# Both MLP products as seven half-size products instead of eight, with the activations kept in DRAM

## The chip, the cores and the metric

The kernel runs on one core of a Trainium2 chip. The metric is the device time of one execution in microseconds (us). Several engines work side by side, each on its own list of instructions: TensorE (PE, matmuls; its weight loads are shown as PEld), VectorE (DVE), ScalarE (ACT), GpSimd (POOL) and SyncE (SP), which here issues the DMA transfers. They wait for each other through semaphores.

## The reference

One decoder layer on 512 tokens of width 2048, in float32: three token mixers, gates, an output projection, and then the part that the change is about. All of it ends in one norm:

```python
x = x + merged @ w_out[l]
h = rmsnorm(x, norm_mlp[l])
x = x + jnp.square(jax.nn.relu(h @ mlp_w1[l])) @ mlp_w2[l]   # 2048 -> 8192 -> 2048
return rmsnorm(x, final_norm)                                # (1, 512, 2048)
```

## The kernel before

Activations are feature-major: a tile holds 128 features on the partitions and the 512 tokens along the free axis, so 16 tiles make up x. A float32 product is made from three products of a reduced type (fp32r): every operand is split exactly into a high and a low half, and hi·hi, hi·lo and lo·hi are added up in PSUM. `wtiles` (L723) brings 512 KB of weights (eight 128x128 tiles) by one DMA into `raw`, ScalarE casts it to `hi` (L731) and VectorE subtracts to get `lo` (L732); each of the three buffers has 3 copies. `gemm` (L735) runs the three matmuls of each weight tile (L748 to L750): the weight tile is stationary, 512 tokens move through.

The stages that matter are the last ones (L1118 to L1210). The output projection makes 16 tiles `wo0` to `wo15`; each is added to x on VectorE, scaled and split into `hh` (high, ScalarE) and `ho` (low, VectorE), and squared for the norm, whose factor R is multiplied in after the first MLP product. The MLP runs in 8 pieces c of 1024 hidden features: 8 tiles of the first product (each 16 weight tiles), ReLU (ScalarE), two multiplications and a split (`ah`, `al`), and then 16 tiles of the second product (each 8 weight tiles), each added to x. The last half piece is run in two halves of the tokens (256 columns), so that the final norm of the first half lies beside the matmuls of the second.

The order of TensorE's instructions is the order of the code (`manual_schedule`). The other engines' lists are ordered by the framework's scheduler from dependences and priorities; weight preparation has a high priority (`wprio`), and buffer counts set how far it runs ahead.

## Time and profile before

| what | us |
|---|---|
| runs: median (lowest to highest), 3 runs | 3062.14 (3059.55 to 3068.38) |
| profiled execution: span | 3059.8 |
| of it: everything up to the last product of w_out | 1646 |
| the MLP's matmuls | 1397 |
| from the last matmul of the MLP on | 17 |

The profile gives the span of one execution, and no time of its own for what lies around it. Its span is 2.3 us below the median of the runs and within their spread. Times in the trace count from the span's start. A row of the timeline is: start, length, engine, line, operation, output<-inputs, count, and in brackets how long the engine was idle before it and what released it. A group's row gives the count, the busy time, the mean length of one in ns and the idle time before them. A matmul's length contains its way through the array; the next one starts earlier, so rates are read from starts.

### The profile page before, as it was taken

What the parts mean: (1) busy time and instruction counts of PE and PEld (TensorE: products, weight loads), DVE (VectorE), ACT (ScalarE), POOL (GpSimd) and SP (SyncE); (2) the same over time, 40 slices, a digit from 0 to 9 for tenths busy, and PEclk for the clock granted to TensorE, in tenths of its full rate; (3) what the DMA queues carried; (4) which work ended last, traced back from release to release, by engine and by line L of the source; (5) the groups of instructions that cost most, each with busy time, mean ns of one, the idle gap of its engine ahead of it and who ended that gap; (6) DMA issues with size and microseconds to landing.
All of it is one profiled execution on the core that took longest, in us unless ns stands there. A gap on an engine that the chain in (4) does not pass through costs nothing.

```text
span 3059.8 us, 36455 instructions
## 1 busy us (share of the span) xinstructions
PE 3001.3 (98%) x14143; PEld 2468.2 (81%) x14143; DVE 1557.3 (51%) x2350; ACT 989.0 (32%) x1224; POOL 336.8 (11%) x572
## 2 busy tenths in 40 slices
PE   8999988999999999999999999999999999999997
PEld 7888776788877777888888888888888888888887
DVE  7766888855664555555334334333333434333335
ACT  6554121234662233422223222122222212222235
POOL 1001766530000000011110000000000000000003
PEclk9999988999999999999999999999999999999999
DMA  5345333445337163655432333333233323323334
GB/s 181 124 162 185 114 103 98 136 131 166 102 103 190 55 186 97 229 165 170 157 98 94 97 99 96 99 98 97 97 97 97 97 96 97 97 96 97 97 97 151
DMA packets 172638, 370.72 MB, mean 121 GB/s; under 512 B 63377, under 2 KB 74385, under 8 KB 171665
## 3 DMA queue, kind: packets, MB, share of 16 engines
q1 hardware_dynamic: 172464, 368.38, 38.2%
q8 instruction: 112, 1.84, 0.3%
q14 instruction: 62, 0.50, 0.1%
HBM read 318.81 MB, written 44.58 MB: 119 GB/s over the span
## 4 chain that ended last, share of the span: by engine, by line
PE 85%; DVE 6%; POOL 3%; DMA 3%; SPq 1%; issue 1%; ACT 0%; DVEq 0%; ACTq 0%; POOLq 0%
PE w L748 15%; PE w L749 15%; PE w L750 15%; PE gt L748 5%; PE gt L750 5%; PE gt L749 5%; PE z L748 2%; PE z L750 2%; PE z L749 2%; PE wo L750 2%; PE up L748 2%; PE wo L748 2%; PE up L750 2%; PE up L749 2%; PE wo L749 2%
## 5 line engine op out<-in xcount | busy, mean ns | idle before, releaser
L731 ACT CAST whw<-wrw 128x1024 fp32r<-128x1024 f32 x264 | 278.0, 1053 | 885.8 <-PE w L749 872.4
L32 DVE TENSOR_TENSOR wlw<-wrw,whw 128x1024 fp32r<-128x1024 f32 x264 | 324.1, 1227 | 405.2 <-ACT whw L731 405.2
L748 PE MATMUL w<-ah,whw 128*128 128x512 f32 (+1 forms) x1088 | 409.9, 377 | 0.1
L750 PE MATMUL w<-ah,wlw 128*128 128x512 f32 (+1 forms) x1088 | 409.7, 377 | 0.0
L749 PE MATMUL w<-al,whw 128*128 128x512 f32 (+1 forms) x1088 | 409.7, 377 | 0.0
L748 PE MATMUL w<-hh,whw 128*128 128x512 f32 x1024 | 398.7, 389 | 0.0
L750 PE MATMUL w<-hh,wlw 128*128 128x512 f32 x1024 | 398.4, 389 | 0.0
L749 PE MATMUL w<-ho,whw 128*128 128x512 f32 x1024 | 398.4, 389 | 0.0
L748 PE MATMUL gt<-uh,whgt 128*128 128x512 f32 x768 | 310.6, 404 | 2.8 <-DVE gz L26 2.8
L750 PE MATMUL gt<-uh,wlgt 128*128 128x512 f32 x768 | 300.6, 391 | 2.0 <-DVE wlgt L32 2.0
L749 PE MATMUL gt<-ul,whgt 128*128 128x512 f32 x768 | 300.2, 391 | 0.0
L29 DVE TENSOR_TENSOR x<-x,w 128x512 f32<-128x512 f32 (+1 forms) x136 | 89.2, 656 | 388.0 <-PE w L750 388.0
L748 PE MATMUL z<-uh,whin 128*128 128x512 f32 x608 | 243.7, 401 | 11.8 <-DVE zs L26 11.8
L750 PE MATMUL z<-uh,wlin 128*128 128x512 f32 x608 | 241.0, 396 | 8.1 <-DVE wlin L32 8.1
L749 PE MATMUL z<-ul,whin 128*128 128x512 f32 x608 | 240.0, 395 | 0.0
L748 PEld LDWEIGHTS w<-ah,whw 128*128 128x128 f32 x1088 | 204.7, 188 | 37.7 <-issue 0.2
L749 PEld LDWEIGHTS w<-al,whw 128*128 128x128 f32 x1088 | 204.7, 188 | 37.5
L750 PEld LDWEIGHTS w<-ah,wlw 128*128 128x128 f32 x1088 | 204.7, 188 | 37.4
L748 PEld LDWEIGHTS w<-hh,whw 128*128 128x128 f32 x1024 | 192.2, 188 | 40.2 <-issue 0.2
L749 PEld LDWEIGHTS w<-ho,whw 128*128 128x128 f32 x1024 | 192.2, 188 | 40.1 <-issue 0.2
L750 PEld LDWEIGHTS w<-hh,wlw 128*128 128x128 f32 x1024 | 192.2, 188 | 39.9
L29 POOL TENSOR_TENSOR acc<-acc,sq 128x512 f32<-128x512 f32 x29 | 49.7, 1713 | 1521.7 <-ACT sq L830 1490.7
(442 smaller groups left out, 4577.8 us busy)
## 6 DMA issues: line engine op xcount, KB each, us to landing
wrw<-in_w SPq DMA_DIRECT2D x264, 512.0 KB, 3.6
wrgt<-in_w_in SPq DMA_DIRECT2D x96, 512.0 KB, 4.0
wrin<-in_w_in SPq DMA_DIRECT2D x76, 512.0 KB, 3.6
wrup<-in_w_up SPq DMA_DIRECT2D x32, 512.0 KB, 4.0
wrwo<-in_w_out SPq DMA_DIRECT2D x32, 512.0 KB, 3.6
gd<-gz SPq DMA_DIRECT2D x48, 256.0 KB, 2.2
gl<-gd SPq DMA_DIRECT2D x48, 256.0 KB, 3.1
zd<-zs SPq DMA_DIRECT2D x21, 256.0 KB, 2.0
```

What stands on the lines that cost most here:

```text
L29: (eng or self.nc.vector).tensor_tensor(out, a, b, ALU.add)
L32: (eng or self.nc.vector).tensor_tensor(out, a, b, ALU.subtract)
L731: nc.scalar.copy(hi, raw)
L748: nc.tensor.matmul(ps, hi[:, ws], xh, start=first, stop=False)
L749: nc.tensor.matmul(ps, hi[:, ws], xl, start=False, stop=False)
L750: nc.tensor.matmul(ps, lo[:, ws], xh, start=False, stop=last)
```

## The change

Both MLP products are cut in 2x2 blocks and formed by the Strassen–Winograd scheme: seven block products in place of eight, from sums of blocks. For a product A·B with blocks A11, A12, A21, A22 of the weights, the sums of weights are built up in one buffer (A11, +A12, +A22, +A21) and a second (B: A22, +A12), each 128x1024 sum being split into high and low as a weight was before (`wsums`).

- The projection `wo` runs in the order 0, 8, 1, 9, ...; `hsums(k)` forms four blocks and four differences or sums of h (128x256 each) in the buffer `hG` and splits seven of them into `hch`, `hcl` (128x1792). This happens for k = 0 to 2 inside the projection, and for k = 3 to 7 behind it, in memory that the projection's operands leave.
- x goes token-major: 64 transposes on TensorE, copies on ScalarE, and 16 DMAs to DRAM (`x1d`); they come back for the second product as `xT0` to `xT3`. The norm's factor is one number per token, R2.
- First product: 32 units u, each with 7 products x 8 weight tiles x 3 matmuls of 256 columns. `w1_out` combines the products, squares the ReLU and stores 512 KB of hidden activations to DRAM (`hid`).
- Second product: token-major. Activations are stationary (128 tokens), weights move (512 columns). For each of 8 pieces c and 2 halves n of the output: 7 products x 2 token tiles x 24 matmuls. `hidden(u)` brings one stored tile back (`aG`, 2 buffers), GpSimd forms the four sums, ScalarE and VectorE split 128x1792 (`ah`, `al`, 6 buffers each). `out2` adds each product from PSUM into xT on VectorE, scaled by R2.
- The final norm is one factor per token; w2 is laid out anew on the host.

Comments and docstrings are dropped as well. The diff, cut to its core:

```diff
+    ORDER = (1, 5, 6, 3, 7, 2, 4)
+    def sums(self, G, hi, lo, eng=None):
+        a21, a11, a22, a12, s1, s2, s3, s4 = (G[:, q] for q in range(8))
+        self.sub(s1, a21, a22, eng)
+        self.sub(s2, s1, a11, eng)
+        self.sub(s3, a11, a21, eng)
+        self.add(s4, s2, a12, eng)
+        self.hl(G[:, 1:].rearrange("p q t -> p (q t)"), hi, lo)
+    def wsums(self, name, B, pool, order=None):
...
+        def acc(c, q):
+            t = self.wp.tile([P, 1024], F32, name=f"w{c}{q}{name}", tag="wraw", bufs=self.wraw)
+            nc.sync.dma_start(t, B[q])
+            self.add(at[c], at[c], t)
+            return at[c]
+        how = {1: lambda: load("A", "11"), 5: lambda: acc("A", "12"), 6: lambda: acc("A", "22"),
+               4: lambda: acc("A", "21"), 3: lambda: load("B", "22"), 7: lambda: acc("B", "12"),
+               2: lambda: load("C", "21")}
+        for i in order or self.ORDER:
+            with self.tc.high_priority(self.wprio):
+                x = how[i]()
...
+                nc.scalar.copy(hi, x)
+                self.sub(lo, x, hi)
+            yield i, hi, lo
+    def w1_out(self, u, i, bank, keep, pool, hid):
+        with self.tc.high_priority(2 * self.wprio):
+            if i in (1, 5, 6):
+                keep[i] = pool.tile([P, 256], F32, name=f"pk{i}_{u}", tag=f"pk{i}", bufs=2)
+                nc.scalar.copy(keep[i], bank[self.BANK[i]])
...
+            if i == 7:
+                self.sub(y[:, 2], keep[5], bank["a"])
...
+            elif i == 4:
+                nc.scalar.copy(y[:, 0], bank["a"])
+                f = y.rearrange("p q t -> p (q t)")
+                self.stt(f, f, 0.0, f, ALU.max, ALU.mult)
+                nc.sync.dma_start(hid, f)
-                    for j in range(NT):
-                        pt = self.gps(f"wo{j}")
-                        self.run(self.gemm(f"wo{j}", d["w_out"][j], [(pt, NT)], m))
-                        self.add(x1[j], x1[j], pt)
...
-                        nc.scalar.activation(hi, x1[j], AF.Copy, scale=col("norm_mlp", j))
-                        self.stt(lo, x1[j], col("norm_mlp", j), hi, ALU.mult, ALU.subtract)
...
+                def hsums(k):
+                    G = fp.tile([P, 8, 256], F32, name=f"hG{k}", tag="hG")
+                    for q in range(2):
+                        nc.scalar.activation(G[:, 2 * q:2 * q + 2].rearrange("p q t -> p (q t)"), x1[k + 8 * q], AF.Copy,
+                                             scale=col("norm_mlp", k + 8 * q))
+                    self.sums(G, *hc[k])
+                for n, j in enumerate(q for k in range(8) for q in (k, k + 8)):
...
+                    if j in (8, 9, 10):
+                        hsums(j - 8)
+                trunk.close()
...
+                for k in range(3, 8):
+                    hsums(k)
...
+                gen = self.wsums("u0", w1_quadrants(0), None, (1, 5, 2, 6, 3, 7, 4))
+                bank, keep = banks(0), {}
+                three = [next(gen) for _ in range(3)]
+                for i, *w in three:
+                    self.w1_mm(bank[self.BANK[i]], i, w, hc, range(3))
...
+                    for i, *w in three:
+                        self.w1_mm(bank[self.BANK[i]], i, w, hc, range(3, 8))
+                        self.w1_out(0, i, bank, keep, mp, hid[0])
...
+                    def hidden(u):
+                        with tc.high_priority(2 * self.wprio):
+                            G = mp.tile([P, 8, 256], F32, name=f"aG{u}", tag="aG", bufs=2)
+                            nc.sync.dma_start(G[:, 0:4].rearrange("p q t -> p (q t)"), hid[u])
+                            r = [mp.tile([P, 1792], F32R, name=f"a{q}{u}", tag=f"a{q}", bufs=6) for q in "hl"]
+                            self.sums(G, *r, nc.gpsimd)
+                        return r
...
+                            if n == 0:
+                                for ph in range(2):
+                                    for _ in range(2):
+                                        i, *w = next(gens[ph])
+                                        for t in range(2):
+                                            mm2(bank[self.BANK[i]][t], i, w, aa, ph, t)
+                                            if ph:
+                                                out2(i, n, bank[self.BANK[i]][t], t)
+                            elif c < 7:
+                                nxt = [hidden(4 * c + 4 + u) for u in range(4)]
+                            for (i, *w), (_, *w1) in zip(*gens):
+                                for t in range(2):
+                                    ps = bank[self.BANK[i]][t]
+                                    mm2(ps, i, w, aa, 0, t)
+                                    mm2(ps, i, w1, aa, 1, t)
+                                    out2(i, n, ps, t)
```

Three places in the engines' lists are spoken of below. The first is VectorE's list at the turn from the output projection to the first MLP product. Before, the last split (`ho15`) and the preparation of weights (`wl...`):

```order
L32 TENSOR_TENSOR wlw1_0_0_13456<-wrw1_0_0_13453,whw1_0_0_13455 128x1024
L42 SCALAR_TENSOR_TENSOR ho11_13170<-x1_2_12342,pcol_75,hh11_13169 128x512
L42 SCALAR_TENSOR_TENSOR ho12_13239<-x1_3_12343,pcol_75,hh12_13238 128x512
L42 SCALAR_TENSOR_TENSOR ho13_13308<-x1_3_12343,pcol_75,hh13_13307 128x512
L42 SCALAR_TENSOR_TENSOR ho14_13377<-x1_3_12343,pcol_75,hh14_13376 128x512
L32 TENSOR_TENSOR wlw1_0_8_13494<-wrw1_0_8_13491,whw1_0_8_13493 128x1024
L29 TENSOR_TENSOR x1_3_12343<-x1_3_12343,wo15_13383 128x512
L32 TENSOR_TENSOR wlw1_1_0_13534<-wrw1_1_0_13531,whw1_1_0_13533 128x1024
L42 SCALAR_TENSOR_TENSOR ho15_13446<-x1_3_12343,pcol_75,hh15_13445 128x512
```

And now, the sums and splits of k = 3 to 7 in `hG` behind the last addition to x (the pieces for k = 5, 6 and 7 follow in the same way):

```order
L30 TENSOR_TENSOR x1_3_12355<-x1_3_12355,wo15_13360 128x512
L33 TENSOR_TENSOR wlu0_2_13541<-wCu0_13538,whu0_2_13540 128x1024
L33 TENSOR_TENSOR hcl3_13431<-hG3_13440,hch3_13430 128x1792
L33 TENSOR_TENSOR hG4_13449<-hG4_13449 128x256 x3
L30 TENSOR_TENSOR hG4_13449<-hG4_13449 128x256
L33 TENSOR_TENSOR hcl4_13433<-hG4_13449,hch4_13432 128x1792
L33 TENSOR_TENSOR hG5_13458<-hG5_13458 128x256 x3
L30 TENSOR_TENSOR hG5_13458<-hG5_13458 128x256
L33 TENSOR_TENSOR hcl5_13435<-hG5_13458,hch5_13434 128x1792
```

One split of 128x512 after `wo15` has become five splits of 128x1792 with the sums of four of them.

The second place is SP's list at the turn from the first to the second product. Before, loads of weights alone:

```order
L728 DMA wrw1_7_0_13945<-in_w1 128x1024
L728 DMA wrw1_7_8_13975<-in_w1 128x1024
L728 DMA wrw2_0_0_0_14015<-in_w2 128x1024
L728 DMA wrw2_0_1_0_14039<-in_w2 128x1024
L728 DMA wrw2_0_2_0_14078<-in_w2 128x1024
```

And now, behind the store of the last hidden tile (`hid31`) and the load of `aG0`, the hidden tile `aG1`, weights, and x and the final norm's factors (1 MB each), and `aG2` (`aG3` follows it):

```order
L1288 DMA aG1_21050<-hid1_13486 128x1024
L791 DMA wAv000_21086<-in_w2 128x1024
L791 DMA wAv001_21123<-in_w2 128x1024
L791 DMA wAv010_21406<-in_w2 128x1024
L791 DMA wAv011_21412<-in_w2 128x1024
L1279 DMA xT0_21028<-x1d0_13517 128x2048
L1279 DMA xT1_21029<-x1d1_13518 128x2048
L1279 DMA xT2_21030<-x1d2_13519 128x2048
L1279 DMA xT3_21031<-x1d3_13520 128x2048
L1281 DMA gfin_21036<-in_final_row 128x2048
L796 DMA wA22v001_21171<-in_w2 128x1024
L1288 DMA aG2_21060<-hid2_13487 128x1024
```

The hidden tiles 2 and 3, needed by the first piece, stand behind ten transfers, five of them of 1 MB, which were not there before.

The third is VectorE's list around the start of piece c = 2 of the second product. Before, at the start of a piece:

```order
L26 TENSOR_TENSOR a31_17197<-a31_17197,R_81 128x512
L26 TENSOR_TENSOR a31_17197<-a31_17197 128x512
L32 TENSOR_TENSOR al31_17202<-a31_17197,ah31_17201 128x512
L29 TENSOR_TENSOR x1_0_12340<-x1_0_12340,w2_3_0_17205 128x512
L32 TENSOR_TENSOR wlw2_3_3_0_17305<-wrw2_3_3_0_17302,whw2_3_3_0_17304 128x1024
L29 TENSOR_TENSOR x1_0_12340<-x1_0_12340,w2_3_1_17206 128x512
```

And now (`wl...` split of a weight sum, `wA...` a sum of weights, `al...` split of hidden tiles, `xT...` a product added to x):

```order
L43 SCALAR_TENSOR_TENSOR xT0_21028<-oa110_21960,R2_13521,xT0_21028 128x512
L30 TENSOR_TENSOR wAv200_22286<-wAv200_22286,wA12v200_22304 128x1024
L33 TENSOR_TENSOR al10_21989<-aG10_21986,ah10_21988 128x1792
L43 SCALAR_TENSOR_TENSOR xT1_21029<-oa111_21961,R2_13521,xT1_21029 128x512
L33 TENSOR_TENSOR al11_21999<-aG11_21996,ah11_21998 128x1792
L33 TENSOR_TENSOR wlv200_5_22308<-wAv200_22286,whv200_5_22307 128x1024
L33 TENSOR_TENSOR wlv201_1_22326<-wAv201_22323,whv201_1_22325 128x1024
L30 TENSOR_TENSOR wAv200_22286<-wAv200_22286,wA22v200_22364 128x1024
L30 TENSOR_TENSOR wAv201_22323<-wAv201_22323,wA12v201_22343 128x1024
L33 TENSOR_TENSOR al12_22569<-aG12_22566,ah12_22568 128x1792
L43 SCALAR_TENSOR_TENSOR xT2_21030<-oa200_22280,R2_13521,xT2_21030 128x512
L33 TENSOR_TENSOR wlv201_5_22347<-wAv201_22323,whv201_5_22346 128x1024
```

After these the list goes on with `xT3`, `wlv200_6`, `al13`, `wAv201` (+A22), `xT0`, `xT1` and `wlv201_6`. Two per-tile steps between matmuls (an addition and a split) have become a mix of sums, splits of weights, splits of hidden tiles and additions to x, in one list.

## Rows read from the trace of the kernel before

**Rows 1.** the page's head.

```profile
span 3059.8 us, 36455 instructions
```

**Rows 2.** windows by stage: us, busy PE PEld DVE ACT POOL, PEclk, DMA, GB/s.

```profile
0.00:1646.00 1646.00, 1603.10 (x7799) 1303.58 (x7800) 1000.36 (x1721) 606.59 (x772) 304.00 (x544) 0.99 0.45 140
1646.00:3043.00 1397.00, 1396.93 (x6342) 1164.16 (x6341) 548.61 (x613) 379.41 (x448) 27.28 (x22) 1.00 0.31 99
3043.00:3060.00 17.00, 1.30 (x6) 0.49 (x4) 8.34 (x17) 3.04 (x5) 5.49 (x7) 0.67 0.49 168
```

**Rows 3.** groups by form of the MLP stage: busy us, mean ns, idle before.

```profile
L748 PE MATMUL w<-hh,whw 128*128 128x512 f32 x1024 | 398.7, 389 | 0.0
L748 PE MATMUL w<-ah,whw 128*128 128x512 f32 x960 | 373.4, 389 | 0.0
L748 PE MATMUL w<-ah,whw 128*128 128x256 f32 x128 | 36.5, 285 | 0.1
L32 DVE TENSOR_TENSOR wlw<-wrw,whw 128x1024 fp32r<-128x1024 f32 x262 | 321.6, 1227 | 404.4 <-ACT whw L731 404.4
L29 DVE TENSOR_TENSOR x<-x,w 128x512 f32<-128x512 f32 x120 | 82.5, 688 | 382.7 <-PE w L750 382.7
L731 ACT CAST whw<-wrw 128x1024 fp32r<-128x1024 f32 x262 | 275.9, 1053 | 880.0 <-PE w L749 872.4 <-PE wo L749 4.4 <-issue 3.2
L810 ACT CAST ah<-a 128x512 fp32r<-128x512 f32 x64 | 39.7, 621 | 136.1 <-DVE a L26 136.1
```

**Rows 4.** timeline of PE, first and 57th of 57 starts with 512 columns.

```profile
2959.73 0.39 PE L748 MATMUL w<-ah,whw 128*128 128x512 f32 x1
...
2972.43 0.39 PE L750 MATMUL w<-ah,wlw 128*128 128x512 f32 x1
```

**Rows 5.** timeline of PE, first and 53rd of 53 starts with 256 columns.

```profile
2999.72 0.28 PE L748 MATMUL w<-ah,whw 128*128 128x256 f32 x1
...
3005.97 0.28 PE L749 MATMUL w<-al,whw 128*128 128x256 f32 x1
```

**Rows 6.** timeline of DVE (start, us) around the start of GpSimd's multiplies.

```profile
3027.63 0.42 DVE L26 TENSOR_TENSOR acc<-acc,acc 128x256 f32<-128x256 f32 x1
3027.97 0.41 DVE L29 TENSOR_TENSOR x<-x,w 128x256 f32<-128x256 f32 x1
3028.64 1.22 DVE L32 TENSOR_TENSOR wlw<-wrw,whw 128x1024 fp32r<-128x1024 f32 x1
3029.77 0.97 DVE L29 TENSOR_TENSOR acc<-acc,sq 128x256 f32<-128x256 f32 x1
3030.99 1.43 DVE L32 TENSOR_TENSOR wlw<-wrw,whw 128x1024 fp32r<-128x1024 f32 x1
```

**Rows 7.** timeline of POOL: the final multiplies of 128x256.

```profile
3028.85 16.08 POOL L26 TENSOR_TENSOR x<-x,rt 128x256 f32<-128x256 f32 x16 [29.64 <-DVE rt L42]
3048.92 3.55 POOL L26 TENSOR_TENSOR x<-x,rt 128x256 f32<-128x256 f32 x4 [3.98 <-DVE rt L42]
```

**Rows 8.** DMA issues of the whole span: KB each, us to landing.

```profile
wrw<-in_w SPq DMA_DIRECT2D x264, 512.0 KB, 3.6
x<-in_xT SPq DMA_DIRECT2D x4, 1024.0 KB, 9.9
```

**Rows 9.** timeline of ACT at the turn from w_out to w1.

```profile
1646.72 0.72 ACT L1137 ACTIVATE hh<-x,pcol 128x512 fp32r<-128x512 f32 x1
1647.35 0.62 ACT L830 ACTIVATE sq<-x 128x512 f32<-128x512 f32 x1
```

**Rows 10.** windows in the mixers' stage, columns as in rows 2.

```profile
435.00:440.00 5.00, 2.91 (x16) 2.75 (x16) 5.00 (x10) 0.66 (x2) 4.84 (x6) 0.74 0.45 153
440.00:445.00 5.00, 4.91 (x19) 4.55 (x20) 2.18 (x2) 0.66 (x2) 4.65 (x16) 0.50 0.39 124
```

**Rows 11.** timeline of the tail.

```profile
3047.49 0.42 DVE L42 SCALAR_TENSOR_TENSOR acc<-rt 128x256 f32<-128x256 f32 x1 [2.21 <-ACT rt L371]
3047.95 0.42 DVE L26 TENSOR_TENSOR acc<-acc,acc 128x256 f32<-128x256 f32 x1
```

More of the change, by code (lines that the diff above doesn't have):

```diff
@@ L1 @@
+import contextlib
 import math
@@ new lines, in main @@
+                x1 = [xq[j // 4][:, j % 4] for j in range(NT)]
+                for q in (0, 2, 1, 3):
+                    nc.sync.dma_start(xq[q], d["xT"][4 * q:4 * q + 4].rearrange("j p t -> p j t"))
+                acc = R
+                def hsums(k):
[4 more added lines that the diff above has]
+                    self.sums(G, *hc[k])
@@ new lines, in main @@
+                pm = self.gps("pms")
+                for t in range(4):
+                    nc.tensor.matmul(pm[:, 2 * t:2 * t + 2], acc[:, t * P:t * P + P], self.onesD[:, 0:2], start=True, stop=True)
+                self.ts(R2, pm[:, 0:8:2], 1e-6, ALU.add)
+                nc.vector.reciprocal(R2, R2)
+                front.close()
+                with mixpool("w1", "right") as mp:
+                    for i, *w in three:
+                        self.w1_mm(bank[self.BANK[i]], i, w, hc, range(3, 8))
+                        self.w1_out(0, i, bank, keep, mp, hid[0])
+                    for i, *w in gen:
+                        self.w1_mm(bank[self.BANK[i]], i, w, hc, range(8))
+                        self.w1_out(0, i, bank, keep, mp, hid[0])
+                    for u in range(1, 32):
+                        bank, keep = banks(u), {}
+                        for i, *w in self.wsums(f"u{u}", w1_quadrants(u), mp):
+                            self.w1_mm(bank[self.BANK[i]], i, w, hc, range(8))
+                            self.w1_out(u, i, bank, keep, mp, hid[u])
```

220 lines of the change are left out of this document (130 added, 90 removed).

## The prediction

> **What bounds the kernel now.** I read the stages first. Up to 1646 us the lists of before and after are the same until the first product of w_out, and little of what follows in that stage moves. The MLP's 1397.00 us hold 1396.93 us of busy TensorE at a granted clock of 1.00 (2.4 GHz), while VectorE is busy for 548.61 us of them, 39%, and ScalarE for 379.41; a tail of 17 us follows [rows 2]. So a matmul taken away here is worth its rate, as long as the other engines keep up. They do now: VectorE's splits of weights are preceded by 404.4 us of idle time, ended by ScalarE's casts, which themselves wait 872.4 us for TensorE to release buffers [rows 3]. That idle VectorE time is what the change spends.
>
> **TensorE's part.** From the first to the 57th start with 512 columns, 12.70 us pass, so one takes 0.2268 us [rows 4]; with 256 columns 52 steps take 6.25 us, 0.1202 us each [rows 5]. Before: 3072 matmuls of 512 columns in the first product (696.7 us), 2880 of 512 and 384 of 256 in the second (653.2 + 46.2 = 699.4 us); counts from [rows 3], three lines alike for each. After: the first product has 32 x 7 x 8 x 3 = 5376 of 256 columns, 646.2 us, so 50.5 us less, not an eighth, since the half as wide matmul costs more than half. The second has 8 pieces x 2 halves x 7 products x 2 token tiles x 12 = 2688 of 512 columns, 609.6 us, 89.8 us less. If all else were hidden, 140 us would be gained.
>
> The Trainium skill ("TensorE: Matmul & The Clock Gate", section "Back-to-back issue gap") gives an isolated gap of N/2.4 + 2.5 ns, 109 ns for 256 columns and 216 for 512. By that the first product would save 77 us (5376 x 0.1092 against 3072 x 0.2158). The two starts measured here are 11 ns longer each, which weighs twice as often on the narrow ones, and I go by the rows.
>
> **VectorE's prices.** 128x1024 from SBUF takes 1.23 us [rows 3] and the next starts 1.13 after it; 128x256 takes 0.42, next after 0.34 [rows 6], next dependent one after 0.46 [rows 11]; 128x512 takes 0.69 [rows 3], so I count 0.60. For 128x1792, which no row has, a straight line through 0.688 and 1.227 gives 2.04, step 1.94; ScalarE's cast by 0.621 and 1.053 gives 1.70 [rows 3]. From below, a split of 1792 can't cost less than the 1.23 of 1024; from above, two of 1024, 2.46. I take the line.
>
> **First product.** Per unit VectorE does 7 splits and 4 sums of 1024, the squared ReLU of 1024 and three additions of 256: 12 x 1.14 + 3 x 0.34 = 14.7 us, beside 168 x 0.1202 = 20.2 us of TensorE. Hidden, but one chain is tight: sum 6 and its split stand in the list behind additions that wait for PSUM. I allow 5 us in all (0 to 15).
>
> **Second product, the crux.** In one half n of a piece TensorE works 168 x 0.2268 = 38.1 us. VectorE has 22 operations of 1024 (14 splits, 8 sums), 25.1 us, and 14 additions from PSUM, 8.4: 33.5 us. In each piece four splits of 1792 come on top, 7.8 us. So VectorE has 74.8 us of work in 76.2: nothing is left for waiting. And it stands badly: all four splits are in the first half. Around the start of a piece (time 0: last matmul of the piece before), the list runs from the addition xT0, which waits for TensorE until -2.72, over a weights' sum and al10 (0.60 + 1.14 + 1.94) to +0.96, then xT1, al11, al12, al13, eight operations of 1024 and four more additions: 3.0 + 5.8 + 9.1 = 17.9 us, to 18.9. TensorE needs the last of these, the low half of sum 6, after 4 x 2.72 + 1.8 = 12.7 us. So at least 6.2 us are lost per piece. On top, al12 waits for a chain that starts only when al10 frees its buffer: DMA 3.6 [rows 8], four GpSimd operations 3.6 to 4.0 (four take 3.55 [rows 7]), a cast 1.70. Against VectorE's own work up to there this leaves two waits that I put at 0.9 and 2.4 us (an estimate from these lengths and the list; nothing to 4 us together). GpSimd contention comes next: with GpSimd running from 3028.85 us, a split takes 1.43 instead of 1.22 and a 128x256 addition of two SBUF inputs 0.97 instead of 0.42 [rows 6, 7]. The operations concerned lose 0.2 each, 1.5 us per piece, together 11 us for each of pieces 1 to 7: 77 us. Lower bound 6.2 (43 us), upper bound below.
>
> A gap in TensorE's work may cost clock. In the mixers' stage, after a stretch with 2.91 us busy of 5, the granted clock was 0.50 (1.2 GHz) in the next 5 us although TensorE was busy for 4.91 [rows 10]. The waits here are of 1 to 3 us in a row of busy groups; I take 1 us per piece, 7 us; nothing to 3 us each. The second halves have 33.5 of 38.1 us, but two splits come 0.1 to 0.4 us before their need: 5 us in all (0 to 12). ScalarE's casts (14 x 1.05, two of 1.70 on the mean: 18 us per half) and GpSimd's 16 operations per piece cost nothing of their own beyond this, beside 38.1 us of matmuls.
>
> **Turn from w_out to the first product.** Here nothing stood still before. Now k = 3 to 7 share one buffer hG, so scaling (0.63 + 0.72 [rows 9]), three dependent sums (0.46 + 0.46 + 0.42, 1.4 with the wake-up), cast 1.70 and split 2.04 come one after another, 6.5 us for each of four, after 5.6 us for the first: 31.8 us. Then 30 matmuls remain (3.6 us). Of the first product's matmuls 72, those of k = 0 to 2 of three products, can run before (8.7 us), so 27 us are lost, and I take 28 for a stretch at half clock (22 to 35).
>
> What I cost at nothing there: 64 transposes, the copies and the 16 stores of x, which lie in that same wait; the sums for k = 0 to 2, about 3.4 us of VectorE each, which lie beside w_out's matmuls in place of the splits `ho`.
>
> **Turn to the second product.** aG2 and aG3 stand on SP's list behind ten transfers. Four loads of 1 MB back to back had a median landing of 9.9 us [rows 8], so some 2.2 us per MB and about 23 us for these, with the weights among them; with sums on GpSimd (8 in 7.1), cast and split, al3 is ready about 36 us after the last store, and the work TensorE can do until then is 48 matmuls, 10.9 us, behind the first hidden tiles. Loss 30 us, and 6 for the first piece's list as above: 36 (25 to 50).
>
> **Tail.** The last norm is per token, with its additions beside matmuls: 11 us for 17, and 3 us of waits in the last group: 14.
>
> **Sum.** 1646 + 28 + 646 + 5 + 610 + 36 + 77 + 7 + 5 + 14 = 3074 us of span, against 3059.8 [rows 1]. The median of the runs before is 2.3 us above its span; I predict 3076.
>
> **Rivals.**
> 1. *TensorE stays the bound* (faster). Weight splits run up to three buffers ahead and the waits in VectorE's list fall into slack that I did not see. For it speaks that VectorE's work fits into the time in every stage. With no loss per piece and both turns at their low ends: 3074 - 89 - 6 - 11 = 2968; with the 6.2 us per piece still lost, 3011. Against it: 74.8 of 76.2 us is no slack.
> 2. *VectorE and GpSimd block each other* (slower still). If each of a piece's 16 GpSimd operations holds VectorE up by 0.55 us, as the 128x256 addition was, that is 8.8 us per piece, 7.3 more than I counted, 58 us: 3134. The Trainium skill ("SBUF — State Buffer", section "SBUF: two separate sides") has it as an exclusive lock between GpSimd and a VectorE operation with two SBUF inputs, where the second waits to the end. As a mechanism of this kernel, 16 x 0.89 = 14.2 us per piece from the uncontended row [rows 7] would make it 102 us more, 3178. The rows bear the lock out in part: 1.43 for 1.22 is far less than a whole 0.89.
> 3. *The loads come late* (slower). Each half of the second product reads 14 loads of 512 KB and, on the mean, two hidden tiles, 8.4 MB in 38.1 us: 220 GB/s where the stage moved 99 [rows 2]. Three raw buffers serve 12 of these loads, so one is used anew every 9.5 us; if a landing grows from 3.6 us towards 6, the sums begin to wait for it. At 0.25 to 0.5 us for each of 224 loads that is 56 to 112 us: 3132 to 3188. Against it: the shares of the DMA engines in [rows 2] are under a half.
>
> **How the numbers follow.** Forecast 0.49 (3045 to 3105), rival 1 0.28, rival 2 0.14, rival 3 0.09. Range 3000 to 3135: below it lie rival 1's best cases, above it the full lock and the late loads. This kernel's measurement can tell 0.3%, 9 us, from no change. Faster than 3053: rival 1 and 0.05 of the forecast, 0.33. Between 3053 and 3071: 0.16. Slower: 0.51.
>
> **What would show it.** Right: w1 units of 20.2 us at clock 1.00; TensorE idle for about 28 us at the first turn, ended by VectorE's hcl; idle behind al2/al3 at the second; per piece one idle stretch of some 10 us in the first half, ended by VectorE's wl splits, and none to speak of in the second. Wrong: VectorE busy below 90% in the second product (rival 1), its 1024 operations well above 1.23 us (rival 2), or idle ended by DMA (rival 3).

## The result, and the profile after

| | median, us (lowest to highest) | ratio to before, 95% interval |
|---|---|---|
| before, 4 runs beside it | 3064.17 (3059.55 to 3068.38) | |
| after, 4 runs | 3110.16 (3105.58 to 3117.95) | 1.015 (1.0132 to 1.0168) |

The change makes the kernel 46 us slower. I had forecast slower, 3076 (3000 to 3135): the side was right, but only under a third of the loss (14 of 46 us). The profiled execution of after, and its windows by stage with the columns of [rows 2]:

```profile
span 3108.5 us, 41754 instructions
```

```profile
0.00:1647.70 1647.70, 1601.89 (x7797) 1302.02 (x7798) 1012.19 (x1726) 607.73 (x767) 303.71 (x544) 0.98 0.45 139
1647.70:1676.60 28.90, 18.23 (x101) 15.33 (x100) 16.93 (x22) 22.57 (x31) 1.72 (x1) 0.67 0.49 175
1676.60:2323.70 647.10, 644.98 (x5350) 639.96 (x5350) 483.65 (x477) 269.59 (x349) 0.00 (x0) 1.00 0.63 206
2323.70:2337.10 13.40, 0.18 (x3) 0.02 (x1) 3.58 (x4) 3.11 (x3) 5.85 (x8) 0.61 0.82 306
2337.10:3085.20 748.10, 670.52 (x2688) 520.90 (x2688) 644.07 (x610) 296.19 (x287) 153.60 (x121) 0.95 0.54 180
3085.20:3108.50 23.30, 0.16 (x1) 0.00 (x0) 12.92 (x25) 8.63 (x16) 0.00 (x0) 0.55 0.44 180
```

In [rows 2] TensorE was busy for all but 0.07 us of the MLP. Now the first product runs as before (644.98 of 647.10 us, clock 1.00), but there is a hole at each turn (rows 2 and 4 here), the second product has 77.6 us without TensorE and a granted clock of 0.95, and the tail is 23.3 us. VectorE is busy for 644.07 of 748.10 us there.

**The first turn.** TensorE's list after the projection, with the bracket naming what ended the idle time, and VectorE's splits beside it:

```profile
1655.66 1.14 PE L1251 MATMUL xt<-cst,x 128*128 128x128 f32 x8 [2.18 <-ACT xs L1253]
1674.89 1.84 PE L1257 MATMUL pms<-cst,R 128*128 128x2 f32 x8 [1.54 <-ACT xs L1253]
1676.59 0.56 PE L817 MATMUL ha<-hch,whu 128*128 128x256 f32 x1
```

```profile
1657.71 2.03 DVE L33 TENSOR_TENSOR hcl<-hG,hch 128x1792 fp32r<-128x1792 f32 x1 [1.85 <-ACT hch L888]
1664.30 2.03 DVE L33 TENSOR_TENSOR hcl<-hG,hch 128x1792 fp32r<-128x1792 f32 x1 [1.81 <-ACT hch L888]
1677.53 2.03 DVE L33 TENSOR_TENSOR hcl<-hG,hch 128x1792 fp32r<-128x1792 f32 x1 [0.39 <-ACT hch L888]
```

Two chains run side by side. The splits come every 6.6 us (1657.71 to 1664.30), as forecast. But TensorE stands in front of the transposes of x, and each group waits for ScalarE's copy of the one before; only behind the last (1674.89) does its list come back to the matmuls, at 1676.59. It reaches those that need the last split when that one ends (1677.53 + 2.03 = 1679.56), 31.8 us after the first product's first matmul.

**The second turn.** TensorE, then SP's issues:

```profile
2337.09 0.79 PE L1299 MATMUL oa<-whv,ah 128*128 128x512 f32 x1 [13.22 <-ACT ah L888]
2358.53 0.80 PE L1299 MATMUL oa<-whv,ah 128*128 128x512 f32 x1 [9.06 <-ACT ah L888]
```

```profile
2325.94 1.25 SPq L1288 DMA_DIRECT2D aG<-hid  x2
2329.73 2.91 SPq L1279 DMA_DIRECT2D xT<-x1d  x4
2338.09 0.33 SPq L796 DMA_DIRECT2D wA22v<-in_w  x1
2340.55 2.26 SPq L1288 DMA_DIRECT2D aG<-hid  x2
```

The third and fourth hidden tiles are asked for at 2340.55, although the queue took its entry before them at 2338.09. The buffers say why: `aG` has two, and the first is free only when `al0` is made, at 2340.53 (read from these times, not tried by itself). Then the load itself takes 11.84 us, where one takes 3.29 at the start of piece c = 1 below. Its place in the chain of waits, and the window in which it is under way (columns as above):

```profile
2340.55 11.84 DMA aG<-hid
```

```profile
2340.50:2352.40 11.90, 8.61 (x23) 6.03 (x23) 9.72 (x9) 3.86 (x4) 0.00 (x0) 0.73 1.01 414
```

The DMA engines have no room there (share 1.01, 414 GB/s). In front of this load stand those of x and of the final norm's factors, 1 MB each, which land one after another, 2.5 us apart, up to 2349.84; it lands at 2352.39. In accum2 (below), where x is asked for behind the third hidden tile, that tile lands in 3.3 us, and the first half of the first piece takes 54.8 us instead of 66.0, among other edits:

```profile
aG<-hid SPq DMA_DIRECT2D x1, 512.0 KB, 3.3
```

**A piece of the second product.** The chain of waits at the start of piece c = 1 (start, length, what; "issue" is time for which the profile shows no wait):

```profile
2443.26 2.04 DVE al L33
2445.30 0.02 issue
2445.32 3.29 DMA aG<-hid
...
2448.74 4.21 POOL aG L33 x3
...
2453.03 1.61 POOL aG L30
...
2454.66 1.71 ACT ah L888
...
2456.39 1.93 DVE al L33
```

From the end of the split that frees the buffer (2445.30) to the end of the next tile's own (2458.32) lie 13 us of DMA, GpSimd, ScalarE and VectorE in turn, and what TensorE waits for stands behind it on VectorE: 

```profile
2460.44 0.79 PE L1299 MATMUL oc<-wlv,ah 128*128 128x512 f32 x1 [2.35 <-DVE wlv L33]
2461.46 0.63 PE L1299 MATMUL oc<-whv,al 128*128 128x512 f32 x1
2461.89 0.63 PE L1299 MATMUL oc<-wlv,ah 128*128 128x512 f32 x1
```

After the wait of 2.35 us a matmul starts every 0.43 us, and the granted clock from 2460.4 to 2466.1 is 0.50 (1.2 GHz):

```profile
2460.40:2466.10 5.70, 5.66 (x13) 4.46 (x14) 5.70 (x5) 0.70 (x2) 3.95 (x2) 0.50 0.35 122
```

From piece 1 on, 7 to 20 matmuls of each first half run so. The rate at full clock, first and 95th of 95 starts, for [rows 4]:

```profile
2486.79 0.39 PE L1299 MATMUL ob<-whv,ah 128*128 128x512 f32 x1
...
2508.73 0.40 PE L1299 MATMUL oa<-whv,al 128*128 128x512 f32 x1
```

21.94 us over 94 steps are 0.2334 us each (0.2327 on the mean over the stage's steps without a wait), against 0.2268 before.

### The profile page after: what moved, and what is told of

It is laid out like the page before. It is cut to its first block, busy times and chain, and to the rows that moved or that the text cites. A ratio compares the mean times of both kernels' runs of the same rounds, so it can differ in the third digit from the quotient of the medians.

```text
span 3108.5 us, 41754 instructions
## 1 busy us (share of the span) xinstructions
PE 2936.0 (94%) x15933; PEld 2478.2 (80%) x15933; DVE 2173.3 (70%) x2863; ACT 1207.8 (39%) x1451; POOL 464.9 (15%) x673
## 3 DMA queue, kind: packets, MB, share of 16 engines
q1 hardware_dynamic: 208000, 507.86, 50.7%
## 4 chain that ended last, share of the span: by engine, by line
PE 70%; DVE 13%; DMA 7%; issue 3%; POOL 3%; ACT 3%; SPq 1%; DVEq 0%; ACTq 0%; POOLq 0%
PE ha L817 11%; PE oa L1299 6%; PE hc L817 5%; PE gt L749 5%; PE gt L751 5%; PE gt L750 5%; PE oc L1299 3%; PE hb L817 3%; PE z L749 3%; PE z L751 2%; PE z L750 2%; DVE wlv L33 2%; PE ob L1299 2%; DMA wA21v<-in_w 2%; PE wo L749 2%
## 5 line engine op out<-in xcount | busy, mean ns | idle before, releaser
L817 PE MATMUL ha<-hch,wlu 128*128 128x256 f32 x1024 | 292.1, 285 | 1.2 <-DVE wlu L33 1.1
L817 PE MATMUL ha<-hch,whu 128*128 128x256 f32 x1024 | 289.1, 282 | 0.9 <-DVE hy L33 0.9
L817 PE MATMUL ha<-hcl,whu 128*128 128x256 f32 x1024 | 289.0, 282 | 0.0
L1299 PE MATMUL oa<-whv,ah 128*128 128x512 f32 x512 | 206.5, 403 | 22.4 <-ACT ah L888 22.3
L1299 PE MATMUL oa<-wlv,ah 128*128 128x512 f32 x512 | 206.5, 403 | 10.2 <-DVE wlv L33 9.3
L807 ACT CAST whv<-wAv 128x1024 fp32r<-128x1024 f32 x128 | 132.9, 1049 | 198.3 <-DVE wAv L30 69.4
L1299 PE MATMUL oa<-whv,al 128*128 128x512 f32 x512 | 205.3, 401 | 4.5 <-DVE al L33 4.5
L33 DVE TENSOR_TENSOR wlu<-wAu,whu 128x1024 fp32r<-128x1024 f32 x128 | 154.0, 1222 | 78.5 <-ACT whu L807 78.5
L817 PEld LDWEIGHTS ha<-hch,wlu 128*128 128x128 f32 x1024 | 194.4, 190 | 5.8 <-DVE wlu L33 2.0
L817 PEld LDWEIGHTS ha<-hch,whu 128*128 128x128 f32 x1024 | 194.1, 190 | 1.1 <-ACT whu L807 1.1
L817 PEld LDWEIGHTS ha<-hcl,whu 128*128 128x128 f32 x1024 | 193.9, 189 | 0.2 <-DVE hcl L33 0.2
```

The lines of the kernel that those rows point to most:

```text
L33: (eng or self.nc.vector).tensor_tensor(out, a, b, ALU.subtract)
L807: nc.scalar.copy(hi, x)
L817: self.nc.tensor.matmul(ps, w[a][:, ws], hc[k][b][:, g], start=i in (1, 5, 2) and k == 0 and q == 0, stop=k == 7 and q == 2, skip_group_ch ...
L1299: nc.tensor.matmul(ps, x[a][:, g], w[b][:, ws], start=i in (1, 5, 2) and ph + p + q == 0, stop=ph + p + q == 4, skip_group_check=True)
```

## The experiments

All ratios are to the kernel before on the same chip (median 3063 to 3066). "Halves" are the times between the first matmuls of the two halves n of each piece; in after the first piece has 66.0 and 40.3, the other seven 45.3 to 53.3 and 39.5 to 40.7. Ranges below are of pieces 1 to 7, and of the second halves without the very last.

**dvesum: no GpSimd.**

```diff
-                            self.sums(G, *r, nc.gpsimd)
+                            self.sums(G, *r, nc.vector)
```

> Only edit: the four sums of each hidden tile in the second product run on VectorE instead of GpSimd. Theory 1 (GpSimd and VectorE hold each other up: VectorE's weight sums take 1.75 us instead of 1.22 beside GpSimd in the changed kernel, and GpSimd's four sums 5.9 us): VectorE gains 0.34 x 16 = 5.4 us of work per piece but loses the holding up and the chain to the third hidden tile gets some 4 us shorter; the first half of a piece falls from 52.6 to 46 to 49 us, the whole to 3065 to 3085. Rival (VectorE's list is simply too long in the first half): the first half stays at 52 to 55 us, the whole at 3105 to 3130.

Measured: 3107.01 us, 1.0141 (1.0125 to 1.0156); first halves 50.7 to 53.1 in the middle pieces. Piece 1 of after, then of dvesum:

```profile
2443.40:2495.90 52.50, 45.15 (x170) 34.14 (x169) 46.88 (x41) 20.07 (x18) 22.54 (x16) 0.90 0.54 180
```

```profile
2444.20:2495.60 51.40, 42.72 (x169) 33.14 (x168) 48.01 (x57) 19.99 (x18) 0.00 (x0) 0.93 0.56 184
```

With GpSimd at 0 instead of 22.54 us the half is 1.1 us shorter. VectorE takes over the 16 sums (0.42 us each) and is busy for only 1.1 us more, because its other operations no longer stretch: over pieces 1 to 7 of after they take 2.9 us per piece longer than here. So contention has a price, a third of the 8.8 us of rival 2, and most of what dvesum saves of it the 16 sums use up. The run excludes the size of rival 2, not contention.

**static_w2: no weight work in the second product.** After its first half, no weight is loaded, summed or split; the last ones are used again.

```diff
-                            gens = [self.wsums(f"v{c}{n}{ph}", bq(ph), mp, order) for ph in range(2)]
+                            if c == n == 0:
+                                gens = [self.wsums(f"v{c}{n}{ph}", bq(ph), mp, order) for ph in range(2)]
+                            else:
+                                gens = [iter([(i, *kept[ph]) for i in order]) for ph in range(2)]
```

> Left out: the loads, sums and splits of the second product's weights from its second half-piece on; all later products use one kept pair of weight tiles, so the result is another one. The hidden tiles' loads, sums and splits and the additions to x stay. Any theory by which VectorE's, ScalarE's or the loads' work for weights holds TensorE up expects every later half at TensorE's own rate: 168 x 0.2327 = 39.1 us, the whole near 3012. If the longer step of 0.2327 us (0.2267 in the kernel before) comes from weights being written beside the matmuls, it falls to 0.2267 and the halves to 38.1 us, the whole near 2997. If it belongs to the form of the matmuls (activations stationary), it stays. If the hidden tiles' chain alone holds TensorE up, the first halves stay above 42 us.

Measured: 3016.96 us, 0.9842 (0.9824 to 0.986); the first half 66.2, every later one up to the last 39.2. Piece 1, first half:

```profile
2446.50:2485.70 39.20, 39.20 (x169) 31.53 (x168) 18.41 (x18) 4.87 (x3) 11.39 (x16) 1.00 0.16 54
```

The hidden chain alone (18.41 us of VectorE, 11.39 of GpSimd) hides whole. So the loss in pieces 1 to 7 needs the work for weights; the second halves of after, which have that work and no hidden splits, lose 0.4 to 1.6 us each. It takes both. The run takes loads, casts, sums and splits away together, and doesn't tell which of them it is. And the step is 0.2333 with no weight being written and DMA at 0.16: neither the writing of weights nor their loads make it longer than the 0.2268 of before.

**t1: the first turn's chain shortened.** `hG` fixed, its split in two parts, the remaining matmuls k by k.

```diff
-                    self.sums(G, *hc[k])
+                    for q0, q1 in ((1, 4), (4, 8)):
+                        c = slice(256 * q0 - 256, 256 * q1 - 256)
+                        self.hl(G[:, q0:q1].rearrange("p q t -> p (q t)"), hi[:, c], lo[:, c])
```

> Only edits, at the turn from the output projection to the first product: one fixed buffer hG whose parts are released one by one, the split done in two parts (blocks, then sums), and the remaining matmuls of the first three products run k by k. Theory (a chain of scaling, sums, cast and split per k through one buffer, 6.5 us each, and 45 matmuls behind the last): per k 3.5 to 4.5 us, 9 matmuls behind the last, so the first unit falls from 49.2 to 33 to 37 us and the whole by 12 to 16 us to about 3096. Rival (TensorE there waits for the transposes' copies on ScalarE, 16 of them about 1.5 us apart): the first unit stays above 44 us.

Measured: 3115.73 us, 1.017 (1.0153 to 1.0187); the first unit 51.5 us instead of 49.2. ScalarE in t1:

```profile
1680.29 0.58 ACT L1262 COPY xs<-xt 128x512 f32<-128x512 f32 x1 [0.90 <-DMA x1d<-xs]
```

My chain did get shorter: the last split ends 27.1 us after the first product's first matmul, 31.8 in after. But TensorE comes back from the transposes only after 29.5 us (28.8 in after). The copies of the transposed x wait for their stores to give back two buffers, and TensorE stands behind them: the second chain holds the turn as long as the first.

**split1: hidden sums and splits in the first product.** High and low halves are stored there, and loaded ready for use.

```diff
+            r = [pool.tile([P, 1792], F32R, name=f"hs{q}{u}", tag=f"hs{q}", bufs=1) for q in "hl"]
+            self.sums(y, *r, self.nc.gpsimd)
+            for q in range(2):
+                nc.sync.dma_start(hid[q], r[q].bitcast(F32))
```

> Edit: the sums and the split of the hidden tiles are made in the first product, right behind the squared ReLU (sums on GpSimd, cast on ScalarE, split on VectorE), and high and low halves are stored; the second product loads both and has 7 buffers of each. Theory (in the second product VectorE's list in the first half of a piece is too long and the chain to the hidden tiles stands across ScalarE's and VectorE's lists): VectorE loses 7.8 us per piece there, GpSimd all its work; the first half falls from 52.6 to 40 to 44 us, the whole by 70 to 110 us to 3000 to 3040, the first product's units stay at 20.2 to 20.6 us. Rival (loads come late): it moves 1.8 MB more per hidden tile each way, near 290 GB/s in both products; then first halves stay above 48 us with waits that end on a DMA, and units grow above 21 us.

Measured: 3240.26 us, 1.0578 (1.0562 to 1.0594); units of the first product 22.7 to 24.4 us, first halves 52 to 56 in the middle pieces (1 to 6). The waits of TensorE in its second product (us in total, times, longest):

```profile
PE oa L1302 <- ACT whv L807: 113.0, 8, 47.7
```

VectorE's splits of hidden tiles are gone from the second product and the wait is still there, 47.7 us at the turn and some 9 us in each later piece: by SP's list, weights now stand behind eight loads of 917 KB per piece (not tried by itself). In the first product, where I had counted slack (14.7 of 20.2 us), the added work costs 3.5 us per unit.

**late: hidden loads tied to the second half's additions.** A one-column copy makes each load wait for a step of the half, so that the hidden splits spread over it.

```diff
-                            elif c < 7:
-                                nxt = [hidden(4 * c + 4 + u) for u in range(4)]
+                                    if t and n and c < 7 and step in (0, 2, 4, 5):
+                                        nxt.append(hidden(4 * c + 4 + len(nxt), x[:, 0:1]))
```

> Only edit: the loads of the next piece's hidden tiles are tied (by a copy of one column) to an addition to x in the second half of a piece, so that the sums, casts and splits of its first two tiles no longer stand in the first half, where TensorE waits; the last two stay there. Theory (VectorE's list is too long in the first half, and ScalarE's casts of weights stand behind the cast of a hidden tile that waits for GpSimd): the first half falls from 52.6 to 43 to 47 us, the second grows from 40.1 to 40 to 42 us, the whole falls by 35 to 60 us to 3050 to 3075. Rival (VectorE's total is the bound, 82 us of work per piece as measured): what the first half gains the second loses, the piece stays above 89 us, the whole above 3090.

Measured: 3141.81 us, 1.0249 (1.0234 to 1.0265); first halves 47.2 to 48.4, second 47.9 to 51.2. Work moved to the other half takes its loss along, and more: 9 us lost for 5 gained.

**best1: late, with three smaller edits.** t1; eight of the sixteen groups of transposes inside the projection; the last norm's factors for two token tiles at a time.

```diff
+                    if n > 7:
+                        xspill((0, 2)[n > 11], n % 4, self.ps(f"xt{n}"))
...
-                        nc.vector.reduce_sum(v, ssq[:, tt], axis=mybir.AxisListType.X)
+                        nc.vector.reduce_sum(v, ssq[:, t0:t0 + 2], axis=mybir.AxisListType.X)
```

> The edit of the late kernel; at the first turn the fixed buffer and the k by k order, and now eight of the sixteen transposes with their copies to DRAM inside the output projection; in the tail the two token tiles of a pair share one logarithm and one exponential. Theory for the turn (two chains end together there: the splits, and the transposes whose copies wait for transfers to DRAM to release a buffer): with half of the transposes gone the first unit falls from 49.2 to 36 to 42 us; rival: it stays above 46, then neither chain sets it. Tail: from the last matmul to the end 23 us before, 16 to 19 us now, since ScalarE loads two tables of 1.28 us instead of four, twice. The whole 15 us under the late kernel, 3035 to 3060.

Measured: 3133.97 us, 1.0223 (1.0199 to 1.0246). The first unit takes 43.0 us (from 49.2), at 3.3 us more in the projection; the tail 17.7 (from 23.3).

**accum: sums of weights by adding DMAs.** GpSimd issues transfers that add to the tile; the hidden sums go to VectorE, and the products in the order 1, 2, 5, 3, 6, 7, 4.

```diff
+            if dma:
+                nc.gpsimd.dma_start(at[c], B[q], accum_op=ALU.add)
+                return at[c]
```

> Edits in the second product alone: the sums of weights are made by transfers that add in place (issued by GpSimd's queue) in place of a load and an addition on VectorE; the sums of hidden tiles go from GpSimd to VectorE; the products run in the order 1, 2, 5, 3, 6, 7, 4, so that two sums of one buffer are not neighbours. VectorE loses 16 additions of 1024 and gains 16 of 256 per piece: from 82 us busy to about 66 of 78. Theory (VectorE's total work with the waits in its list is what bounds the second product): the piece falls from 92.3 to 80 to 85 us, the whole to 3010 to 3050. Rival (what bounds is the chain to the hidden tiles and the order of the lists, not VectorE's total): first halves stay above 49 us, the whole above 3085. A third way: adding transfers take much longer than the plain ones' 3.6 us; then TensorE's and ScalarE's waits end on these transfers and the piece grows past 92 us.

Measured: 3093.39 us, 1.0088 (1.0071 to 1.0105); second halves 39.0 to 39.2, first halves 49.4 to 50.9 in the middle pieces; the very last half, in an order of its own, 51.5 (39.6 in accum2, in the order of the others). The loads of the first tiles and the adding ones (issues, KB, us to landing), and ScalarE at the start of a piece:

```profile
wAv<-in_w POOLq DMA_DIRECT2D x96, 512.0 KB, 5.8
wAv<-in_w SPq DMA_DIRECT2D x32, 512.0 KB, 3.9
```

```profile
2641.34 1.04 ACT L810 CAST whv<-wAv 128x1024 fp32r<-128x1024 f32 x1 [8.54 <-DMA wAv<-in_w]
```

With the sums off VectorE the second halves are at TensorE's own time. The first ones still wait: the adding DMA can start only when the sum before it is split, and that split stands behind hidden splits.

**best2: accum, late and the three edits together**, with x loaded between the hidden tiles.

> The accum kernel and, beside it: the next piece's hidden tiles tied to the second half of a piece (as in late); the turn and the tail of best1; the last half in the same order of products; at the turn to the second product the four loads of x (1 MB each) wait for the sums of the hidden tiles 1 and 3, and the final norm's factors for the second piece. Theory (in the first halves VectorE's list is too long, and moving work to the second halves costs there only as long as VectorE has no room: with 27 of 40 us busy in the accum kernel it has): first halves fall from 49.5 to 41 to 46 us, second halves stay at 39.2 to 40.5; the first half of all from 60 to 70 us to 50 to 58; the tail 18 us, the last half 41; the whole 3010 to 3050, so faster than the kernel before (3064). Rival (the order of the lists at the start of a piece sets the loss whatever their load): the piece stays at 88 us and the whole above 3070.

Measured: 3090.29 us, 1.0079 (1.0065 to 1.0093); first halves 48.6 to 51.0, second 40.5 to 44.6.

**best3: best2 with the hidden sums in the first product** (stored, 917 KB a tile), so that only the split is left.

```diff
+        if i == 4:
+            self.sums(y, None, None, nc.gpsimd)
+            nc.sync.dma_start(hid, y[:, 1:].rearrange("p q t -> p (q t)"))
```

> The best2 kernel with two further edits: the sums of the hidden tiles are made in the first product by GpSimd, which is idle there, and stored (917 KB per tile for 512); the second product has 7 buffers of high and low halves in place of 6 (one buffer aG less, and the final norm's factors loaded for the last piece into it), so that three of a piece's four hidden tiles are ready before it begins, and the loads are tied to the first four products of a second half. Theory (two things together set the loss at the start of a piece: VectorE's room, which the adding transfers gave, and the chain from a released buffer to the third hidden tile, 4.4 and 1.8 us of waiting in each first half of best2): first halves fall from 49 to 40 to 43 us, second halves 39.2 to 41, units of the first product 20.2 to 20.6; the whole 3030 to 3055, faster than the kernel before. Rival (GpSimd's sums in the first product hold VectorE up there, as the split did): units grow above 20.8 us, 20 us or more in all. Second rival: first halves stay above 46 us, then the order of the casts and splits at the start of a piece sets them, not the buffers.

Measured: 3225.68 us, 1.0541 (1.0516 to 1.0566); first halves 41.7 to 44.4, second 53.6 to 59.2, units of the first product 20.3 to 25.0. TensorE's waits in its second product:

```profile
PE oa L1318 <- DVE xT L1331: 65.9, 7, 10.8
```

The first halves do what I meant. But an addition to x now stands in VectorE's list behind a hidden split whose buffer TensorE itself must first give back: about 10 us per piece.

**best4 and accum2: best2 with the ties earlier, and without any.**

```diff
-                                    if t and n and c < 7 and step in (0, 2, 4, 5):
+                                    if t and n and c < 7 and step in (0, 1, 2, 3):
```

> As best2 (weight sums by adding DMAs, two rows of transposes inside the output projection, joint tail, x loaded between the hidden tiles), but the four hidden loads of a piece are tied to the first four steps of the second half in place of steps 0, 2, 4 and 5. Theory (in best2 the first halves of 48 to 50 us wait because the third and fourth hidden tile come late): first halves 41 to 45 us, second halves 41 to 44, a piece 83 to 87, whole 3030 to 3065. Rival (VectorE's list: whatever is split earlier delays the additions to x that stand behind it): first halves gain 4 to 6 us and second halves lose as much, a piece stays at 90 to 92, whole 3080 to 3100.

> best2 without the tie of the hidden loads: adding DMAs, hidden sums on VectorE, hidden loads asked for ahead of the second half as in the changed kernel. It tells whether the tie or the adding DMAs give best2 what it has over accum. Theory (the tie is worth nothing once the weight sums are off VectorE): second halves 39.2, first halves 49 to 51, a piece 89 as in accum, first half 60 and tail 18 as in best2, whole 3075 to 3085. Rival (the tie helps): 3095 or more.

Measured: best4 3078.2 us, 1.0036 (1.0022 to 1.0051), first halves 40.4 to 46.7, second 45.4 to 49.9; accum2 3065.96 us, 1.001 (1.0001 to 1.0018), first halves 45.1 to 50.4, second 39.0 to 39.4. Pieces 1 to 6 take 88.6 us on the mean in both: in best4 the third and fourth hidden tile come in time, as meant, and the second half loses as much. The tie only moves the loss, now for the fourth time (late, best1, best2, best4, all with the same kind of tie), and accum2 does without it.

**best5: accum2 with a fourth pair of buffers** for the high and low halves of weights.

```diff
-                hi = self.wp.tile([P, 1024], F32R, name=f"wh{name}_{i}", tag="whi", bufs=self.whl)
+                own = dma and self.nw % 4 == 0
+                hp, hb, ht = (pool, 1, "x") if own else (self.wp, self.whl, "")
+                hi = hp.tile([P, 1024], F32R, name=f"wh{name}_{i}", tag="whi" + ht, bufs=hb)
```

> accum2 with a fourth pair of buffers for the high and low halves of weights in the second product (the memory comes from gfin, which takes a buffer of the hidden tiles in the last piece). In accum2 the second halves are at TensorE's own 39.0 us and the first halves at 50, with waits for the cast of an added-up weight tile (3.3 to 3.8 us) and for the split behind it (2.2 us) that follow the hidden splits in VectorE's list. Theory (weights are prepared only as far ahead as three buffers allow, so a stretch of hidden splits reaches TensorE at once): with a fourth, first halves 43 to 47 us, second halves 39.0, whole 3015 to 3045. Rival (the chain of sums through one buffer and the adding DMA sets the time, and more buffers behind it change nothing): first halves 49 to 51, whole 3060 to 3072.

Measured: 3040.84 us (3036.51 to 3043.91), 0.9926 (0.9913 to 0.994): 0.7% faster than the kernel before, and 2.2% faster than after. TensorE's waits from piece 1 on in accum2, then in best5, and the two halves of piece 1 of best5:

```profile
PE oc L1314 <- ACT whv L810: 23.4, 8, 3.6
PE oc L1314 <- DVE wlv L33: 14.4, 11, 2.1
```

```profile
PE oa L1316 <- DVE xT L1329: 21.5, 7, 4.1
PE oc L1316 <- DVE xT L43: 6.1, 7, 1.2
PE oc L1316 <- DVE wlv L33: 0.5, 1, 0.5
```

```profile
2431.20:2476.10 44.90, 41.14 (x170) 32.56 (x170) 39.21 (x49) 19.74 (x19) 7.76 (x9) 0.96 0.82 211
2476.10:2515.00 38.90, 38.90 (x169) 31.50 (x168) 26.13 (x29) 15.44 (x15) 6.03 (x7) 1.00 0.84 189
```

The waits for weights are all but gone at the same work for VectorE (39.21 us here; in accum2's 50.4 us long half 39.41): between these two kernels how far weights ran ahead set the time, not how much there was to do. On after itself, where VectorE is busy for 81.8 of a piece's 92 us, the fourth pair wasn't tried. What is left is a wait for additions to x, some 4 us per piece.

Between the spans of after and best5 lie 69.4 us. By the stage times of the two traces: 6.7 from the first product, less 3.7 in the projection and 1.4 before it; 10.5 from the first piece with its turn; 50.9 from pieces 1 to 7 (641.7, 616.0 in accum2, 590.8: half from accum2's edits and half from the fourth buffers); 6.5 from the tail.

## Why the prediction was right in its side and short in its size

The sum stood at 3074, the span is 3108.5. Two slips of arithmetic don't touch it: 5376 x 0.1092 against 3072 x 0.2158 is 76 us and not 77, and 5.6 + 4 x 6.5 is 31.6 and not 31.8. Term by term; half-clock steps are counted in the trace, and waits are what is left of a half beyond 168 steps of 0.2327 and these:

| term | forecast | measured |
|---|---|---|
| to the last product of w_out | 1646 | 1647.7 |
| first turn and first product | 679 | 676.0 |
| second product, TensorE alone | 610 | 625.5 |
| first piece with its turn, beyond that | 36 | 41 |
| waits in the first halves of pieces 1 to 7 | 77 | 68 |
| half clock in them | 7 | 20 |
| second halves | 5 | 7 |
| tail | 14 | 23.3 |

- *The step of the second product* was mis-sized, 16 us. I took the 0.2268 of [rows 4] for a form in which activations stand and weights move; it takes 0.2327, for 2688 matmuls (12 per product and token tile, not the 24 named in the list of the change). Every row I used has the weights standing, so none excluded it, and I gave this term no bounds. That was the error. The Trainium skill ("TensorE: Matmul & The Clock Gate", section "Back-to-back issue gap") gives an isolated gap of N/2.4 + 2.5 ns, a formula in N alone, 216 ns at 512 columns; the measured 233 and 227 disagree with it and with each other. Why the step is longer stays open. In best5, with the same roles, it alternates from product to product between 0.2309 and 0.2330, so the roles alone don't set it, and the buffer may have a part; that was not tried.
- *The clock* was mis-sized, 13 us: I took 1 us per piece and had 3 as the upper end. Measured is 2.8 on the mean (14 matmuls of a first half at 0.43 instead of 0.233). The clock was at 0.50 once or twice in each first half; in piece 1 that came after waits of 2.27 and 2.35 us. In piece 4 the first wait is as long (2.28), and the granted clock behind it is 1.00:

```profile
2726.80:2732.00 5.20, 5.17 (x22) 4.06 (x22) 5.00 (x3) 0.00 (x0) 5.12 (x4) 1.00 0.42 135
```

- *The waits per piece* were right in cause and about right in size: VectorE's list, with hidden splits ahead of weight splits and the `aG` chain in it. 11 us were forecast, 9.7 measured (67.9 over 7). Of the 57.4 us that TensorE idles in pieces 1 to 7, 46.3 end on a split of weights. That the waits need the work for weights is shown by static_w2 (none when weights stand still); that it is the list they share with the hidden splits is read from these releasers. That their cause is a full list was only half of it. VectorE was busy for 81.8 of 92 us in a piece, but in accum2 for only 65.6 of 89.6, and there 10 us per piece were still lost; a fourth pair of buffers took away over a third of that (88.0 to 84.4 us per piece, where TensorE alone needs 78) at the same VectorE work. I had taken three buffers of run-ahead as given and never asked what a fourth was worth. My sign for rival 1, VectorE busy below 90%, came up (644.07 of 748.10 us, 86%) without rival 1 being true: a busy share doesn't tell who waits.
- *The second turn* was right in its cause: hidden tiles behind 1 MB transfers. `aG2` landed 26.8 us after the last store was issued (23 forecast for the transfers before it), and `al3` was ready after 36.9 us (36). I overlooked that SP's order isn't all: the two `aG` buffers hold the request back until 2340.53, 2.5 us behind the entry before it. How 36 us less 10.9 of work became a loss of 30 the prediction doesn't say. Of the 5 us missing in the whole, 3.9 are half clock, which I hadn't counted there.
- *The first turn* has the right size (the first unit takes 49.2 us instead of 20.2, 29.0 for 28), and the chain of splits the forecast 31.8, but this is half the cause: I had set the transposes at nothing, "in that same wait", and they are a second chain of the same length. t1 shows it: shortening my chain gained nothing. I had also let 72 matmuls of the first unit run before the wait; it is 27 (3 k x 3 matmuls x 3 products). Two errors that met the right size are luck in part.
- *The tail* was mis-sized, 9 us. The last matmul's products are added at 3091.77, behind 3.67 us of the other tiles' scaling, and then ScalarE's table loads, which [rows 11] don't show, come twice for each token tile:

```profile
3088.19 3.67 DVE L43 SCALAR_TENSOR_TENSOR xT<-xT,tot,gfin 128x1024 f32<-128x1024 f32 x3
3091.77 0.75 DVE L43 SCALAR_TENSOR_TENSOR xT<-oa,R,xT 128x512 f32<-128x512 f32 x1
```

```profile
3093.36 1.28 ACT L371 ACT_TABLE_LOAD   x1
3094.87 1.28 ACT L372 ACT_TABLE_LOAD   x1
```

The rivals. *TensorE stays the bound* is wrong for after, and what static_w2 (3017) and best5 (3041) come nearer to it: the distance is above all the work for weights. *VectorE and GpSimd block each other* was too dear, not wrong. A weights' sum beside GpSimd takes 1.75 us instead of 1.22, and a GpSimd operation beside it 1.71 instead of 0.72:

```profile
2333.22 0.72 POOL L33 TENSOR_TENSOR aG<-aG 128x256 f32<-128x256 f32 x1
...
2449.57 1.71 POOL L33 TENSOR_TENSOR aG<-aG 128x256 f32<-128x256 f32 x1
...
2450.61 1.75 DVE L30 TENSOR_TENSOR wAv<-wAv,wA22v 128x1024 f32<-128x1024 f32 x1
2452.28 1.75 DVE L30 TENSOR_TENSOR wAv<-wAv,wA12v 128x1024 f32<-128x1024 f32 x1
```

They take turns, one of each in 1.67 us, so the trace bears out the lock that the Trainium skill states ("SBUF — State Buffer", section "SBUF: two separate sides") in the main, though a pair takes less than 1.22 + 0.72. VectorE loses 0.53 us each time. But only some of a piece's 16 operations meet one of VectorE with both inputs in SBUF (an addition to x, from PSUM, takes 0.74 beside GpSimd as without): 2.9 us per piece, for the 1.5 I counted and rival 2's 8.8. *The loads come late*: 180 GB/s were moved in the second product (I had said 220) at a DMA share of 0.54, and from piece 1 on none of TensorE's waits ended with a load; in the first piece the load of `aG2` was late, as shown above. In accum, where loads add, the cast that TensorE waits for does wait for one.

## What to carry to other kernels

A saving on the engine that bounds a stage is worth what the next engine's *order and run-ahead* leave of it, not what its busy time leaves: with VectorE at 66 of 90 us a piece still lost 10, and one more pair of buffers took over a third of that away at the same busy time. Before work is moved about within a period, see what a buffer more would do; moving it, in four kernels, only moved the wait. And a rate read from one form of a matmul holds for that form: with the operands' roles exchanged it is a price that no row has, and wants bounds like any other.

## What was not expected of the hardware

- fp32r matmuls of 512 columns with activations standing start every 0.2327 us, with weights standing every 0.2268; with no weights being written (static_w2) it is 0.2333.
- A DMA that adds 512 KB to SBUF lands 5.8 us after its issue, a plain one in the same kernel after 3.9, and its issue takes GpSimd 0.86 us.
- After a wait of 2.35 us between busy stretches 13 matmuls (5.7 us) ran at a granted clock of 0.50; after one of 2.28 us in piece 4, 22 ran at 1.00.
- A GpSimd operation on 128x256 and a VectorE sum on 128x1024, both with two inputs in SBUF, take turns: 1.71 us for 0.72 and 1.75 for 1.22.
